# Two edits in a conformer decoder trunk on one core: an unused tile of 256 in place of 384 bytes, and a half layer norm's mean and root computed in PSUM by column

## The chip, the cores and the metric

The kernel runs on one core of one Trainium2 chip. Its time is the device time of that core in microseconds (us); the reported time is the median over several executions. Before the change it is 1984.59 us, the median of 3 (1982.06 to 1985.19). TensorE (PE in the profile) multiplies matrices out of SBUF into PSUM; VectorE (DVE), ScalarE (ACT) and GpSimd (POOL) work element by element; the queue of SyncE (SP) issues most of the DMAs. SBUF and PSUM both have 128 partitions; the addresses below are bytes within a partition.

## The reference

Two macaron layers over 512 tokens of 1024 channels, in fp32. Layer 0 mixes tokens with a convolution, layer 1 with stick-breaking attention; each layer has a half-step gated feed-forward block before and after its mixer.

```python
for layer in range(2):
    h = h + 0.5 * swiglu_ffn(rms_norm(h, ffn1_norm[layer]), ...)     # 1024 -> 2816 -> 1024
    u = rms_norm(h, mix_norm[layer])
    if layer == 0:                                                   # conformer_conv
        a, gate = split(u @ w_pw1 + b_pw1); c = a * sigmoid(gate)
        c = causal_depthwise_conv(c, w_dw, width=31) + b_dw
        c = silu(layer_norm(c, ln_g, ln_b))                          # mean and variance over channels
        h = h + c @ w_pw2 + b_pw2
    else:
        h = h + stick_breaking_attention(u @ wq, k, v) @ wo          # 16 heads of 64
    h = h + 0.5 * swiglu_ffn(rms_norm(h, ffn2_norm[layer]), ...)
    if layer == 0: k, v = split(rms_norm(h, kv_norm) @ w_kv)
return rms_norm(h, final_norm)
```

## The kernel before

The activations stand transposed: 8 chunks of 128 channels, each a tile of 128 partitions by 512 tokens. Each fp32 operand of a matmul is split into a high and a low part (`split`: ACT casts to the high part, DVE subtracts it for the low part), and a product takes three matmuls (`mm3`, L325 to L327): weight high by x high, weight high by x low, weight low by x high. The weight is the stationary operand (128x128, loaded by PEld), the activation the moving one (128x512).

There are four feed-forward blocks (`ffn`, called here blocks 0 to 3). Each runs in thirds of 8, 8 and 6 hidden chunks f. For each f two products, gate and up, go into PSUM tiles `pg` (8 input chunks by 3 matmuls each); DVE and ACT make the hidden tile from them and split it into `hhi` and `hlo`. After a third, each of the 8 output chunks d takes a product `pd` over the third's hidden tiles. The moving operand of `pg` is `xhi`/`xlo` of a `Norm`, that of `pd` is `hhi`/`hlo`. Weights come in units of 128x1024 (`unit`, `fetch`) through three buffers each of `raw`, `whi` and `wlo`.

Where tiles lie: pools are laid out one after the other, `const`, `wp` (weights), `xp` (the `xhi`/`xlo` of blocks 0, 2 and 3), `tp`, then the pools of each stage. `lean(tp, LEAN_TP)` reserves a tile in `tp` that nothing writes or reads; `LEAN_DG` does so in a later pool. What lies behind it in `tp`, and each later pool, starts higher by its size. In the built program the tiles of interest start, modulo 512 bytes:

| tiles | before | after |
|---|---|---|
| `whi`, `wlo`; `xhi`, `xlo` of blocks 0, 2, 3 and of the mixers (up to byte 105536) | 64 | 64 |
| `xhi`, `xlo` of block 1 (pool `x2`); `hhi`, `hlo`, `tg`, `tu` (all blocks); `kvh`, `kvl`, `oh`, `ol` (attention) (from byte 107968 on) | 192 | 64 |
| `qs`, `ks`, `sh`, `sl`, `wh`, `wl`, `vs` (attention); `sq` and diagonals (`dg`) in `tp` | 448 | 320 |
| `gl`, `glh`, `gll` (convolution, four buffers each) | 0, 128, 256, 384 | 64, 192, 320, 448 |

The convolution stage is not left to the scheduler but written as steps for a planner (`Plan`): each step has an engine, an estimated duration, its buffers and a rank, and `issue` orders the steps by a list schedule over these estimates. First come the projections `pa` with the gate (`gl`); then, for each channel chunk, 31 taps shared between PE (diagonal matrices `d` into PSUM tiles `pc`), ACT and POOL (`pr`, `ws`) and DVE (L690, adding onto `pc`). The last three chunks are done in two halves of 256 tokens, so that the layer norm of the first half, `layer_norm(0, ..)`, can begin while the taps of the second half still run.

`layer_norm(h, ..)` sums over channels with matmuls: `ms` holds the mean of 2 x 128 tokens in 2 columns of a PSUM tile, `mq` the mean square. DVE copies the mean to the SBUF tile `sm` (L713). `row` then brings two columns onto all partitions: split them (L719, L720), scale an identity by each part on ACT (`dg_lm`, `dg_lr`, L726) and multiply by ones on PE (`pb_lm`, `pb_lr`, L728). `variance` (L736 to L740) squares the mean, subtracts, clamps, and takes the inverse root with `inv_root` (L360 to L370: two integer instructions, then three rounds of three). With both rows there, DVE and POOL subtract the mean (L746, L748), DVE multiplies by the root (L756), ACT applies Silu (L757) and casts (L759), and `second` multiplies by the weights of the second projection (`pp`).

Attention is left to the scheduler, which orders it by its own model of time: projections (`pk`, `pq`, `pv`), 16 heads (`z`, `av`), and the output projection (`po`).

Of the kernel before, what the change touches and what calls it, by code (L numbers as in the profile page):

```python
# [30 lines left out]
LEAN_TP, LEAN_DG = 384, 64  # L31
# [151 lines left out]
def decoder_kernel(ctx, tc, xin, gu, dna, dnb, pw1, pw2, kq, wv, wo, out):  # L183
# [343 lines left out]
    with ExitStack() as c:  # L527
# [125 lines left out]
        def depthwise(ch, sl, rank):  # L653
# [18 lines left out]
            for t in range(n_pe, n_pe + n_pool):  # L672
                q = ch * KW + t
                x, g = lambda t=t: gl()[:, t + h : t + sl.stop], col("w_dw", q)
                if t > n_pe:
                    pr = held("pr", f"pr{q}_{h}", [P, T], F32)
                    add("A", 0.6 * f + 0.08 * half, lambda pr=pr, x=x, g=g: A.activation(pr()[:, at0], x(), AF.Copy, scale=g),  # L677
# [3 lines left out]
                else:  # L681
                    add("A", 0.6 * f + 0.08 * half, lambda x=x, g=g: A.activation(
# [21 lines left out]
        def layer_norm(h, rank):  # L704

            sl, n = TOKENS[h], T // 2
            sm = cv.tile([P, 8], F32, name=f"sm{h}")
            mean, var, root = sm[:, 0:2], sm[:, 2:4], sm[:, 4:6]
            y7, sq = ("y", NC - 1, sl.start), ends[h]
            ms, mq = bank(f"ms{h}", 2), bank(f"mq{h}", 2)  # L710
            add("PE", 1.0, lambda: token_sums(ms(), dsum[:, sl], y[NC - 1]()[:, sl]), r=[f"dsum{h}", y7], w=[ms], rank=rank)
            add("PE", 1.0, lambda: token_sums(mq(), dsq[:, sl], sq()[:, sl]), r=[f"dsq{h}", sq], w=[mq], rank=rank)
            add("V", 0.2, lambda: V.tensor_copy(mean, ms()), r=[ms], w=[("mean", h)], rank=rank)  # L713

            def row(name, small, key):
# [403 lines left out]
```

## Time and profile before

| | |
|---|---|
| time, median of 3 | 1984.59 us |
| the profiled execution: its own time | 1984.59 us |
| its span in the profile | 1982.8 us |
| PE busy | 1938.9 us, 98% |
| DVE busy | 1089.9 us, 55% |
| ACT busy | 787.8 us, 40% |
| POOL busy | 278.4 us, 14% |

Busy shares are means over stages with different limits. A matmul's record lasts longer than the distance to the next matmul's start, since they are pipelined, so a sum of records says little and starts say more. The stages, in us from the span's start: block 0 to 372, convolution to 583, block 1 to 953, block 2 to 1316, attention to 1625, block 3 to the end.

### The profile page before, as it was taken

To read this page: it belongs to the slowest core of one execution; us is meant where nothing else is said; L and a number is where in the kernel's file an instruction comes from. 1 tells how busy PE (TensorE), PEld (TensorE's weight loads), DVE (VectorE), ACT (ScalarE), POOL (GpSimd) and SP (SyncE) were. 2 spreads that over 40 slices of the span, in tenths; PEclk is the share of its full clock that TensorE was granted. 3 is DMA by queue.
4 is the path that set the end of the run, shared out by engine and by line. 5 is a ranking of instruction groups with operands and counts; after the bars stand their busy time and mean duration, and the time that the engine had idled before them with its cause. 6 is when DMAs were issued, how large, how long until landed. Compare 5 with 4: busy or idle time off the path is not lost.

```text
span 1982.8 us, 23270 instructions
## 1 busy us (share of the span) xinstructions
PE 1938.9 (98%) x8991; PEld 1594.9 (80%) x8993; DVE 1089.9 (55%) x1646; ACT 787.8 (40%) x1222; POOL 278.4 (14%) x261
## 2 busy tenths in 40 slices
PE   8999999999799999999999999999999999999997
PEld 6888888888788888888888888888888688888885
DVE  6444534599754434345743443467989754344344
ACT  5424323667543222223422322346777633222222
POOL 0212202099500000000000000003453100000000
PEclk9999999999899999999999999999999999999998
DMA  5757746443243232322333333242323132332321
GB/s 195 242 172 241 270 144 230 166 159 128 107 160 96 94 91 92 96 93 89 105 97 94 97 97 95 76 157 77 86 76 93 57 96 96 96 96 87 105 83 66
DMA packets 69630, 237.62 MB, mean 120 GB/s; under 512 B 7952, under 2 KB 8080, under 8 KB 69520
## 3 DMA queue, kind: packets, MB, share of 16 engines
q1 hardware_dynamic: 62032, 209.93, 33.1%
q10 hardware_dynamic: 7488, 26.22, 3.6%
q8 instruction: 70, 1.15, 0.2%
q14 instruction: 40, 0.33, 0.1%
HBM read 202.56 MB, written 29.36 MB: 117 GB/s over the span
## 4 chain that ended last, share of the span: by engine, by line
PE 88%; DVE 5%; ACT 3%; issue 1%; POOL 1%; DMA 1%; SPq 0%; DVEq 0%; POOLq 0%; ACTq 0%
PE pg L327 16%; PE pg L325 16%; PE pg L326 16%; PE pd L327 8%; PE pd L326 8%; PE pd L325 8%; PE z L946 1%; DVE pc L690 1%; PE pa L326 1%; PE pa L327 1%; PE pa L325 1%; PE po L325 1%; PE po L326 1%; PE po L327 1%; POOL ws L679 1%
## 5 line engine op out<-in xcount | busy, mean ns | idle before, releaser
L234 ACT CAST whi<-raw 128x1024 fp32r<-128x1024 f32 (+2 forms) x305 | 313.0, 1028 | 940.8 <-PE pg L326 376.9
L325 PE MATMUL pg<-xhi_f,whi 128*128 128x512 f32 x1408 | 550.3, 391 | 4.2 <-ACT xhi_f L390 1.7
L326 PE MATMUL pg<-xlo_f,whi 128*128 128x512 f32 x1408 | 550.1, 391 | 1.6 <-DVE xlo_f L391 1.6
L327 PE MATMUL pg<-xhi_f,wlo 128*128 128x512 f32 x1408 | 550.0, 391 | 0.1
L235 DVE TENSOR_TENSOR wlo<-raw,whi 128x1024 fp32r<-128x1024 f32 (+2 forms) x305 | 368.6, 1210 | 63.9 <-ACT whi L234 63.6
L325 PEld LDWEIGHTS pg<-xhi_f,whi 128*128 128x128 f32 x1408 | 264.3, 188 | 64.0 <-ACT whi L234 3.9
L326 PEld LDWEIGHTS pg<-xlo_f,whi 128*128 128x128 f32 x1408 | 264.3, 188 | 60.1 <-DVE xlo_f L391 3.0
L327 PEld LDWEIGHTS pg<-xhi_f,wlo 128*128 128x128 f32 x1408 | 264.3, 188 | 57.6 <-DVE wlo L235 0.8
L326 PE MATMUL pd<-hlo,whi 128*128 128x512 f32 x704 | 277.4, 395 | 0.0
L327 PE MATMUL pd<-hhi,wlo 128*128 128x512 f32 x704 | 276.8, 395 | 0.0
L325 PE MATMUL pd<-hhi,whi 128*128 128x512 f32 x704 | 276.7, 395 | 0.0
L464 DVE SCALAR_TENSOR_TENSOR xpar<-pd,xpar 128x512 f32<-128x512 f32 x96 | 66.0, 691 | 256.9 <-PE pd L327 256.9
L448 DVE TENSOR_TENSOR tu<-pg,r_f 128x512 f32<-128x512 f32 x88 | 60.8, 691 | 265.8 <-PE pg L327 265.6
L446 DVE TENSOR_TENSOR tg<-pg,r_f 128x512 f32<-128x512 f32 x88 | 60.8, 691 | 179.9 <-PE pg L327 179.9
L326 PEld LDWEIGHTS pd<-hlo,whi 128*128 128x128 f32 x704 | 132.1, 188 | 32.2
L327 PEld LDWEIGHTS pd<-hhi,wlo 128*128 128x128 f32 x704 | 132.1, 188 | 32.0
L325 PEld LDWEIGHTS pd<-hhi,whi 128*128 128x128 f32 x704 | 132.2, 188 | 32.0
L845 POOL TENSOR_SCALAR_AFFINE_SELECT tri<-ones 128x128 f32<-128x128 f32 x1 | 0.3, 294 | 725.3 <-DVE tu L449 725.3
L235 POOL TENSOR_TENSOR plo<-praw,phi 128x1024 fp32r<-128x1024 f32 x24 | 57.5, 2400 | 283.4 <-ACT phi L234 281.8
L679 POOL TENSOR_TENSOR ws<-ws,pr 128x256 f32<-128x256 f32 (+1 forms) x90 | 90.8, 1019 | 28.3 <-ACT pr L677 24.6
L690 DVE SCALAR_TENSOR_TENSOR pc<-gl,xpar,pc 128x512 f32<-128x512 f32 (+1 forms) x154 | 91.9, 639 | 2.8 <-PE pc L669 1.1
L234 ACT CAST hhi<-tu 128x512 fp32r<-128x512 f32 x88 | 54.9, 624 | 67.1 <-DVE tu L449 67.1
(262 smaller groups left out, 2489.6 us busy)
## 6 DMA issues: line engine op xcount, KB each, us to landing
raw<-in_gu_dram SPq DMA_DIRECT2D x175, 512.0 KB, 3.5
raw<-in_dna_dram SPq DMA_DIRECT2D x64, 512.0 KB, 3.5
whi<-aparth SPq DMA_DIRECT2D x29, 512.0 KB, 3.5
wlo<-apartl SPq DMA_DIRECT2D x29, 512.0 KB, 4.4
praw<-in_pw_dram SPq DMA_DIRECT2D x24, 512.0 KB, 4.0
aparth<-phi ACTq DMA_DIRECT2D x24, 512.0 KB, 2.7
apartl<-plo ACTq DMA_DIRECT2D x24, 512.0 KB, 3.8
raw<-in_dnb_dram SPq DMA_DIRECT2D x32, 384.0 KB, 3.1
```

The lines of the kernel that those rows point to most:

```text
L234: ins = A.copy(dst_hi, src)
L235: (G if on_pool else V).tensor_sub(dst_lo, src, dst_hi.bitcast(F32))
L325: PE.matmul(ps, w[0], x[0], start=first, stop=False)
L326: PE.matmul(ps, w[0], x[1], start=False, stop=False)
L327: PE.matmul(ps, w[1], x[0], start=False, stop=last)
L446: V.tensor_mul(tg, pt[0], rb)
L448: V.tensor_mul(tu, pt[1], rb)
L464: V.scalar_tensor_tensor(res[d], pd, 0.5, res[d], op0=ALU.mult, op1=ALU.add)
L679: add("G", 1.28 * f + 0.1 * half, lambda pr=pr: G.tensor_add(accp, accp, pr()[:, at0]), r=[pr], w=[at_], rank=rank)
L690: add("V", 0.66 * f + 0.06 * half, lambda x=x, q=q: V.scalar_tensor_tensor(pc(), x(), q, pc(), op0=ALU.mult, op1=ALU.add), r=[gl], w=[pc], ...
L845: G.affine_select(out=tri, in_=ones, compare_op=ALU.is_ge, fill=0.0, base=0, pattern=[[-1, P]], channel_multiplier=1,)
L946: PE.matmul(dst, st, m[:, a:b], start=False, stop=True, skip_group_check=True)
```

## The change

`LEAN_TP` goes from 384 to 256. `layer_norm` loses the SBUF tile `sm` and its copy: `mq` becomes a PSUM tile of 8 columns, of which 0 and 1 take the mean square, 2 and 3 the variance, 4 and 5 the root, 6 and 7 a scratch value. `row` takes its two columns from PSUM (`ms`, and columns 4 and 5 of `mq`). The products of two columns become two instructions on one column each, with the other factor as a scalar by partition, also in PSUM. `inv_root`, still used by the RMS norms, has its first two instructions in a function of their own. Five estimates of the planner change (one is shown).

```diff
-LEAN_TP, LEAN_DG = 384, 64
+LEAN_TP, LEAN_DG = 256, 64
...
+    def first_root(y, v):
+
+        V.tensor_scalar(y.bitcast(I32), v.bitcast(I32), 1, None, op0=ALU.logical_shift_right)
+        V.tensor_scalar(
+            y.bitcast(I32), y.bitcast(I32), -1, 0x5F3759DF, op0=ALU.mult, op1=ALU.add
+        )
...
-                add("A", 0.54, do, w=[d], rank=rank)
+                add("A", 0.6, do, w=[d], rank=rank)
...
-            sm = cv.tile([P, 8], F32, name=f"sm{h}")
-            mean, var, root = sm[:, 0:2], sm[:, 2:4], sm[:, 4:6]
...
-            ms, mq = bank(f"ms{h}", 2), bank(f"mq{h}", 2)
+            ms, mq = bank(f"ms{h}", 2), bank(f"mq{h}", 8)
...
-            add("V", 0.2, lambda: V.tensor_copy(mean, ms()), r=[ms], w=[("mean", h)], rank=rank)
...
-                    V.tensor_copy(parts[:, :2], small)
-                    V.tensor_sub(parts[:, 2:], small, parts[:, :2].bitcast(F32))
+                    V.tensor_copy(parts[:, :2], small())
+                    V.tensor_sub(parts[:, 2:], small(), parts[:, :2].bitcast(F32))
...
-            lm = row("lm", mean, ("mean", h))
+            lm = row("lm", ms, [ms])
...
             def variance():
-                V.tensor_mul(root, mean, mean)
-                V.tensor_sub(var, mq(), root)
+                var, root, t = (mq()[:, a : a + 2] for a in (2, 4, 6))
+                one = [slice(j, j + 1) for j in range(2)]
+                for j in one:
+                    V.tensor_scalar_mul(root[:, j], ms()[:, j], ms()[:, j])
+                for j in one:
+                    V.tensor_scalar(var[:, j], root[:, j], -1.0, mq()[:, j], op0=ALU.mult, op1=ALU.add)
                 V.tensor_scalar(var, var, 0.0, LN_EPS, op0=ALU.max, op1=ALU.add)
-                inv_root(root, var, f"ln{h}")
-            add("V", 2.9, variance, r=[mq, ("mean", h)], w=[("root", h)], rank=rank)
-            lr = row("lr", root, ("root", h))
+                first_root(root, var)
+                for _ in range(3):
+                    for j in one:
+                        V.tensor_scalar_mul(t[:, j], root[:, j], root[:, j])
+                    for j in one:
+                        V.tensor_scalar(t[:, j], t[:, j], var[:, j], -0.5, op0=ALU.mult, op1=ALU.mult)
+                    for j in one:
+                        V.tensor_scalar(root[:, j], t[:, j], 1.5, root[:, j], op0=ALU.add, op1=ALU.mult)
+            add("V", 3.4, variance, r=[ms], w=[mq], rank=rank)
+            lr = row("lr", Buf("-", lambda: mq()[:, 4:6]), [mq])
```

On DVE, the first layer norm from the mean's arrival to the first round of the root, before (`sm` is the SBUF tile, a tap of the second half's convolution reads `gl` into `pc_256`):

```order
L713 COPY sm_2889<-ms_4309 128x2 [waits PE_49]
L690 SCALAR_TENSOR_TENSOR pc_256_4166<-gl_3758,xpar,pc_256_4166 128x256 [waits DVE_49]
L719 CAST dp_lm_2890<-sm_2889 128x2 [waits DVE_49]
L720 TENSOR_TENSOR dp_lm_2890<-sm_2889,dp_lm_2890 128x2 [waits DVE_49]
L690 SCALAR_TENSOR_TENSOR pc_256_4166<-gl_3758,xpar,pc_256_4166 128x256
L737 TENSOR_TENSOR sm_2889<-sm_2889 128x2
L738 TENSOR_TENSOR sm_2889<-mq_4322,sm_2889 128x2 [waits DVE_49,PE_49]
L739 TENSOR_SCALAR sm_2889<-sm_2889 128x2 [waits DVE_49]
L363 TENSOR_SCALAR sm_2889<-sm_2889 128x2 [waits DVE_49]
L364 TENSOR_SCALAR sm_2889<-sm_2889 128x2 [waits DVE_49]
L368 TENSOR_TENSOR rt_ln_4347<-sm_2889 128x2 [waits DVE_49]
L369 SCALAR_TENSOR_TENSOR rt_ln_4347<-sm_2889,rt_ln_4347 128x2 [waits DVE_49]
```

and the same place now:

```order
L722 CAST dp_lm_2889<-ms_4315 128x2 [waits PE_49]
L723 TENSOR_TENSOR dp_lm_2889<-ms_4315,dp_lm_2889 128x2 [waits DVE_49]
L694 SCALAR_TENSOR_TENSOR pc_256_4159<-gl_3759,xpar,pc_256_4159 128x256
L743 TENSOR_SCALAR mq_4328<-ms_4315 128x1 [waits PE_49]
L743 TENSOR_SCALAR mq_4328<-ms_4315 128x1 [waits DVE_49]
L745 TENSOR_SCALAR mq_4328<-mq_4328 128x1 [waits DVE_49] x2
L746 TENSOR_SCALAR mq_4328<-mq_4328 128x2 [waits DVE_49]
L362 TENSOR_SCALAR mq_4328<-mq_4328 128x2 [waits DVE_49]
L363 TENSOR_SCALAR mq_4328<-mq_4328 128x2 [waits DVE_49]
L750 TENSOR_SCALAR mq_4328<-mq_4328 128x1 [waits DVE_49] x2
L752 TENSOR_SCALAR mq_4328<-mq_4328 128x1 [waits DVE_49] x2
L754 TENSOR_SCALAR mq_4328<-mq_4328 128x1 [waits DVE_49] x2
```

The copy is gone, one tap moved ahead of the mean's split, and the products by columns stand in pairs. On PE, the end of the first layer norm's place in the queue, before (`pc_256` are the last diagonal taps of the second half):

```order
L728 MATMUL pb_lm_4372<-dg_lm_0_4339,onesr 128x256
L325 MATMUL pc_256_4257<-glh_4024,d_4239 128x256
L326 MATMUL pc_256_4257<-gll_4039,d_4239 128x256
L327 MATMUL pc_256_4257<-glh_4024,d_4239 128x256
L728 MATMUL pb_lm_4372<-dg_lm_1_4359,onesr 128x256
L669 MATMUL pc_256_4257<-y0h,mshift 128x256
L728 MATMUL pb_lr_4406<-dg_lr_0_4396,onesr 128x256
L728 MATMUL pb_lr_4406<-dg_lr_1_4399,onesr 128x256
L325 MATMUL pp_0_4436<-shi_4419,whi_3767 128x256
```

and now:

```order
L325 MATMUL pc_256_4249<-glh_4022,d_4267 128x256
L326 MATMUL pc_256_4249<-gll_4040,d_4267 128x256
L327 MATMUL pc_256_4249<-glh_4022,d_4267 128x256
L731 MATMUL pb_lm_4383<-dg_lm_0_4339,onesr 128x256
L673 MATMUL pc_256_4249<-y0h,mshift 128x256
L731 MATMUL pb_lm_4383<-dg_lm_1_4379,onesr 128x256
L731 MATMUL pb_lr_4416<-dg_lr_0_4406,onesr 128x256
L731 MATMUL pb_lr_4416<-dg_lr_1_4409,onesr 128x256
L325 MATMUL pp_0_4446<-shi_4430,whi_3765 128x256
```

The last three diagonal taps moved ahead of the mean's row; in both orders no tap is left between the rows of mean and root but the closing one with `mshift`. In attention, PE's queue in the first heads, before (`pq` a projection, `z` the scores of a head):

```order
L327 MATMUL pq_10586<-xhi_mix_4_9878,wlo_10457 128x512
L325 MATMUL pq_10586<-xhi_mix_5_9911,whi_10456 128x512
L326 MATMUL pq_10586<-xlo_mix_5_9912,whi_10456 128x512
L327 MATMUL pq_10586<-xhi_mix_5_9911,wlo_10457 128x512
L946 MATMUL z_0_10275<-sh_0_10295,ntri 128x512
L325 MATMUL pq_10586<-xhi_mix_6_9944,whi_10456 128x512
L326 MATMUL pq_10586<-xlo_mix_6_9945,whi_10456 128x512
L327 MATMUL pq_10586<-xhi_mix_6_9944,wlo_10457 128x512
L946 MATMUL z_1_10281<-sh_1_10321,ntri 128x384
```

and now:

```order
L960 MATMUL z_0_10291<-sh_0_10311,ntri 128x512
L327 MATMUL pq_10602<-xhi_mix_4_9894,wlo_10473 128x512
L325 MATMUL pq_10602<-xhi_mix_5_9927,whi_10472 128x512
L326 MATMUL pq_10602<-xlo_mix_5_9928,whi_10472 128x512
L327 MATMUL pq_10602<-xhi_mix_5_9927,wlo_10473 128x512
L960 MATMUL z_0_10291<-sl_0_10312,ntri 128x512
L960 MATMUL z_0_10291<-sh_0_10311,none 128x256
L960 MATMUL z_0_10291<-sl_0_10312,none 128x256
L325 MATMUL pq_10602<-xhi_mix_6_9960,whi_10472 128x512
```

The head's matmuls stand four places earlier among those of the projection; such shifts run through the whole of attention.

## Rows read from the trace of the kernel before

**Rows 1.** The page's chain of work that ended last, by engine.

```profile
PE 88%; DVE 5%; ACT 3%; issue 1%; POOL 1%; DMA 1%; SPq 0%; DVEq 0%; POOLq 0%; ACTq 0%
```

**Rows 2.** Stretches: length, busy us (instructions) by engine, clock, DMA share, GB/s.

```profile
28.00:372.00 344.00, 344.00 (x1504) 281.99 (x1503) 160.53 (x199) 123.31 (x144) 57.55 (x24) 1.00 0.61 205
372.00:583.00 211.00, 195.42 (x1134) 173.11 (x1132) 167.32 (x333) 139.98 (x306) 121.37 (x129) 0.96 0.40 148
583.00:953.00 370.00, 370.00 (x1591) 298.03 (x1592) 167.51 (x217) 105.14 (x129) 0.00 (x0) 1.00 0.30 94
...
1316.00:1625.00 309.00, 299.32 (x1569) 247.34 (x1571) 242.48 (x419) 193.38 (x352) 93.41 (x92) 0.98 0.28 81
```

**Rows 3.** PE groups by line, block 1: count, busy us, mean ns, idle.

```profile
L325 PE MATMUL pg<-xhi_f,whi 128*128 128x512 f32 x352 | 138.9, 395 | 0.0
...
L326 PE MATMUL pd<-hlo,whi 128*128 128x512 f32 x176 | 69.4, 395 | 0.0
```

**Rows 4.** PE groups by line, block 2.

```profile
L325 PE MATMUL pg<-xhi_f,whi 128*128 128x512 f32 x342 | 133.2, 389 | 0.0
...
L325 PE MATMUL pd<-hhi,whi 128*128 128x512 f32 x176 | 69.2, 395 | 0.0
```

**Rows 5.** PE timeline, first matmuls of thirds in blocks 1 and 2: start, duration.

```profile
711.55 0.40 PE L325 MATMUL pg<-xhi_f,whi 128*128 128x512 f32 x1
...
801.15 0.40 PE L325 MATMUL pd<-hhi,whi 128*128 128x512 f32 x1
...
845.95 0.40 PE L325 MATMUL pg<-xhi_f,whi 128*128 128x512 f32 x1
...
1080.06 0.39 PE L325 MATMUL pg<-xhi_f,whi 128*128 128x512 f32 x1
...
1167.12 0.40 PE L325 MATMUL pd<-hhi,whi 128*128 128x512 f32 x1
```

**Rows 6.** PE's waits in the convolution stage: us in total, times, longest.

```profile
PE pb_lr L728 <- ACT dg_lr L726: 7.6, 1, 7.6
```

**Rows 7.** DVE timeline around the first layer norm: start, us, instructions.

```profile
492.56 8.45 DVE L690 SCALAR_TENSOR_TENSOR pc<-gl,xpar,pc 128x256 f32<-128x256 f32 x21
...
502.69 0.15 DVE L713 COPY sm<-ms 128x2 f32<-128x2 f32 x1
...
504.97 0.37 DVE L737 TENSOR_TENSOR sm<-sm 128x2 f32<-128x2 f32 x1
...
511.96 0.65 DVE L370 SCALAR_TENSOR_TENSOR sm<-rt_ln,sm 128x2 f32<-128x2 f32 x1
...
512.86 0.16 DVE L719 CAST dp_lr<-sm 128x2 fp32r<-128x2 f32 x1
```

**Rows 8.** ACT and POOL timelines in the same stretch.

```profile
507.85 0.51 ACT L677 ACTIVATE pr<-gl,xpar 128x256 f32<-128x256 f32 x1 [0.25 <-POOL ws L679]
513.05 1.28 ACT L726 ACTIVATE dg_lr<-ident,dp_lr 128x128 fp32r<-128x128 f32 x4 [4.69 <-DVE dp_lr L719]
...
510.52 2.07 POOL L679 TENSOR_TENSOR ws<-ws,pr 128x256 f32<-128x256 f32 x3
```

**Rows 9.** DVE timeline around the second layer norm.

```profile
536.75 0.16 DVE L720 TENSOR_TENSOR dp_lm<-sm,dp_lm 128x2 fp32r<-128x2 f32 x1
536.83 0.15 DVE L737 TENSOR_TENSOR sm<-sm 128x2 f32<-128x2 f32 x1
...
539.62 0.16 DVE L370 SCALAR_TENSOR_TENSOR sm<-rt_ln,sm 128x2 f32<-128x2 f32 x1
```

**Rows 10.** Stretches behind the first layer norm's wait, columns as in rows 2.

```profile
514.00:523.50 9.50, 7.47 (x31) 6.89 (x32) 9.37 (x25) 8.35 (x22) 1.60 (x2) 0.50 0.01 2
523.50:527.00 3.50, 3.50 (x31) 3.50 (x31) 1.86 (x6) 1.04 (x3) 2.90 (x5) 1.00 0.00 0
```

**Rows 11.** PE's waits in attention, the longest.

```profile
PE pq L325 <- DVE qt L908: 3.1, 1, 3.1
```

**Rows 12.** The stretch around that wait, columns as in rows 2.

```profile
1340.00:1350.00 10.00, 6.87 (x19) 5.08 (x18) 4.91 (x7) 3.93 (x6) 0.00 (x0) 0.66 0.39 106
```

More of the change, by code (lines that the diff above doesn't have):

```diff
@@ L358, in token_sums @@
                           start=i + b == 0, stop=i == len(src) - 1, skip_group_check=True)
-    def inv_root(y, v, name):
-        t = tp.tile([P, v.shape[-1]], F32, name=f"rt_{name}", tag="rt", bufs=1)
+    def first_root(y, v):
         V.tensor_scalar(y.bitcast(I32), v.bitcast(I32), 1, None, op0=ALU.logical_shift_right)
@@ L366, in inv_root @@
         )
+    def inv_root(y, v, name):
+        t = tp.tile([P, v.shape[-1]], F32, name=f"rt_{name}", tag="rt", bufs=1)
+        first_root(y, v)
         for _ in range(3):
@@ L676, in depthwise @@
                     pr = held("pr", f"pr{q}_{h}", [P, T], F32)
-                    add("A", 0.6 * f + 0.08 * half, lambda pr=pr, x=x, g=g: A.activation(pr()[:, at0], x(), AF.Copy, scale=g),
+                    add("A", 0.6 * f + 0.1 * half, lambda pr=pr, x=x, g=g: A.activation(pr()[:, at0], x(), AF.Copy, scale=g),
                         r=[gl], w=[pr], rank=rank)
@@ L681, in depthwise @@
                 else:
-                    add("A", 0.6 * f + 0.08 * half, lambda x=x, g=g: A.activation(
+                    add("A", 0.6 * f + 0.1 * half, lambda x=x, g=g: A.activation(
                         accp, x(), AF.Identity, scale=g, bias=col("b_dw", ch)), r=[gl], w=[at_], rank=rank)
@@ L706, in layer_norm, with row @@
             sl, n = TOKENS[h], T // 2
-            sm = cv.tile([P, 8], F32, name=f"sm{h}")
-            mean, var, root = sm[:, 0:2], sm[:, 2:4], sm[:, 4:6]
             y7, sq = ("y", NC - 1, sl.start), ends[h]
-            ms, mq = bank(f"ms{h}", 2), bank(f"mq{h}", 2)
+            ms, mq = bank(f"ms{h}", 2), bank(f"mq{h}", 8)
             add("PE", 1.0, lambda: token_sums(ms(), dsum[:, sl], y[NC - 1]()[:, sl]), r=[f"dsum{h}", y7], w=[ms], rank=rank)
-            add("PE", 1.0, lambda: token_sums(mq(), dsq[:, sl], sq()[:, sl]), r=[f"dsq{h}", sq], w=[mq], rank=rank)
-            add("V", 0.2, lambda: V.tensor_copy(mean, ms()), r=[ms], w=[("mean", h)], rank=rank)
-            def row(name, small, key):
+            add("PE", 1.0, lambda: token_sums(mq()[:, 0:2], dsq[:, sl], sq()[:, sl]), r=[f"dsq{h}", sq], w=[mq], rank=rank)
+            def row(name, small, r):
                 parts = tp.tile([P, 4], F32R, name=f"dp_{name}{h}", tag=f"dp{name}{h}", bufs=1)
@@ L718, in part @@
                 def part():
-                    V.tensor_copy(parts[:, :2], small)
-                    V.tensor_sub(parts[:, 2:], small, parts[:, :2].bitcast(F32))
-                add("V", 0.4, part, r=[key], w=[("parts", name, h)], rank=rank)
+                    V.tensor_copy(parts[:, :2], small())
+                    V.tensor_sub(parts[:, 2:], small(), parts[:, :2].bitcast(F32))
+                add("V", 0.5, part, r=r, w=[("parts", name, h)], rank=rank)
                 for i in range(2):
@@ L756, in layer_norm @@
                 add("V", 0.36, lambda yc=yc: V.tensor_mul(yc(), yc(), lr()), r=[lr], w=[yt], rank=rank)
-                add("A", 0.4, lambda yc=yc, ch=ch: A.activation(
+                add("A", 0.5, lambda yc=yc, ch=ch: A.activation(
                     yc(), yc(), AF.Silu, scale=col("ln_g", ch), bias=col("ln_b", ch)), w=[yt], r=["silu"], rank=rank)
-                add("A", 0.4, lambda yc=yc, hi=hi: A.copy(hi()[:, sl], yc()), r=[yt], w=[("shi", ch, h)] + [hi] * (h == 0), rank=rank)
+                add("A", 0.32, lambda yc=yc, hi=hi: A.copy(hi()[:, sl], yc()), r=[yt], w=[("shi", ch, h)] + [hi] * (h == 0), rank=rank)
                 add("V", 0.36, lambda yc=yc, hi=hi, lo=lo: V.tensor_sub(lo()[:, sl], yc(), hi()[:, sl].bitcast(F32)),
```

## The prediction

> **What bounds the kernel now.** I read the chain of work that ended last, then the busy time by stage, then TensorE's starts in each feed-forward block, then the one long wait.
>
> The chain is 88% TensorE [rows 1]. By stage [rows 2], TensorE is busy without a gap in the feed-forward blocks (344.00 of 344.00 us in the first, 370.00 of 370.00 in the second), while the convolution stage leaves 211.00 − 195.42 = 15.6 us idle and attention 309.00 − 299.32 = 9.7. So in four fifths of the span the time is the number of matmuls times the distance between their starts, and only something that changes that distance counts. In the convolution and attention stages DVE is loaded too (167 of 211 us, 242 of 309).
>
> The distance is not the same everywhere. In block 1 a 128x512 matmul lasts 395 ns in both pg and pd [rows 3]; in block 2 pg lasts 389 and pd 395 [rows 4]. Records overlap, so I take the distance from starts. Eight units f make 8 x 2 x 8 x 3 = 384 pg matmuls, eight units d make 8 x 8 x 3 = 192 pd matmuls. In block 1, pg from 711.55 to 801.15 is 89.60 us, 233.3 ns each; the pd behind it, to 845.95, is 44.80 us, again 233.3. In block 2, pg from 1080.06 to 1167.12 is 87.06 us, 226.7 ns [rows 5]. Same engine, shape, clock (1.00 in both), same weights' place; block 1's xhi and xlo begin at 192 modulo 512, block 2's at 64, and hhi and hlo (pd's moving operand) at 192 in every block. So a moving operand at 192 costs 6.6 ns a matmul against one at 64, or something that goes with it does.
>
> **The change part by part.**
>
> *The unused tile.* It puts hhi, hlo, and block 1's xhi and xlo at 64. pd: 4 blocks x 22 x 8 x 3 = 2112 matmuls; pg of block 1: 44 x 8 x 3 = 1056. Together 3168 x 6.6 ns = 20.9 us, all on the path since TensorE has no gap there. What could be late next: DVE has 167.51 busy of 370 us and the DMA engines a share of 0.61 at most in these stages [rows 2], so neither takes over for 2%. Bounds: 0 (the distance goes with another property than the start) to 20.9.
>
> In attention pk and po (192 matmuls each) go from 192 to 64 too: at 6.6 ns the 384 are worth 2.5 us. po has little beside it, pk is mixed with the heads. The tiles of the heads go from 448 to 320, for which no row has a price. I take 1.5 us, between 0 and 2.5. gl, read by DVE and ScalarE, moves through the same four remainders in another order; I take nothing.
>
> *The layer norm's statistics.* For the first half of the tokens TensorE waits once, 7.6 us, for the diagonals of the root (pb_lr) [rows 6]. What it waits for is a string of DVE instructions on two columns [rows 7]: the copy of the means at 502.69, the squaring at 504.97, and the split of the root at 512.86. From 504.97 to 512.61 stand 14 tiny instructions, most at 0.65 to 0.68 us. In the second half the same 14 take 536.83 to 539.78, 0.20 each [rows 9]. The difference is POOL: it adds 256 columns at 0.69 us each until 512.6 in the first half [rows 8] and nothing in the second; DVE's instruction with SBUF on both sides goes through once per POOL instruction. Those with an operand in PSUM do not wait: the copy from ms at 502.69 took 0.15 beside a busy POOL [rows 7].
>
> After the change all of it stands in PSUM. The copy goes; the two instructions of the mean's split read PSUM, 0.2 each; one tap of 8.45 / 21 = 0.40 follows [rows 7]; the string then begins at 502.69 + 0.4 + 0.4 = 503.5, 1.5 earlier. It has 11 pairs of columns and 3 of both, 25 in place of 14. No row shows a PSUM-to-PSUM instruction of one column with a scalar by column. From below: an independent one follows its forerunner after 0.08 (536.75 to 536.83) [rows 9], 25 x 0.08 = 2.0 us. From above: a tap, which reads and writes PSUM, takes a scalar by column and waits for its forerunner, but over 256 columns, 0.40 [rows 7]: 10.0 us. I take 0.20 + 0.08 + 0.07 for a pair and 0.2 for a single, 11 x 0.35 + 0.6 = 4.45 us, nearest to the second half's row. The string ends at 507.95, and with one subtraction of 0.33 before it the root's split starts at 508.3, 4.6 earlier than 512.86.
>
> What is late next is ScalarE. In the new order two products pr stand ahead of the root's diagonals, and pr waits for POOL (507.85, idle 0.25 before it) [rows 8]: 507.85 + 0.51 + 0.69 = 509.05 in place of 513.05. So the gain is 4.0 us, from −1.0 (string of 10.0: 503.5 + 10.0 + 0.33 = 513.8 against 512.86) to 4.3, ScalarE's floor with a shorter wait for POOL. Behind the wait TensorE ran at a granted clock of 0.50, that is at 1.2 GHz: 31 matmuls in 7.47 busy us where the next 31 took 3.50 [rows 10]. It had stood idle before that; with about half the idle I count 1.0 of these 4.0 us back (0 to 4).
>
> By the Trainium skill, SBUF — State Buffer, section "Who interferes with whom", DVE instructions with two SBUF inputs, and those in a two-port mode, wait for the whole of a GpSimd instruction that reads SBUF, and PSUM operands are outside that. By that rule none of the 25 waits, and the trace agrees so far (0.15 us for the copy from PSUM, 0.65 for SBUF to SBUF); were the rule narrower than that, rival 2 is what follows.
>
> In the second half pb_lr has no wait (the one wait of 7.6 is the first half's) [rows 6]: TensorE has pp matmuls beside it, and a string 1.5 us longer than 2.95 hides there; without cover it would cost 1.5.
>
> *The planner's numbers.* They move instructions by a few places from the convolution's start. Until the first layer norm TensorE or DVE is full either way, and each executes the same instructions less the copy; I take nothing, ±1.
>
> *Attention's order.* The scheduler emits its matmuls in another order, though the code there is untouched; SP's queue holds the same DMAs, some of the qs and ks copies one weight load later or earlier. Nothing says which order is better; 0, and ±6 for the bounds, about what the one long pause there costs now (5.7 us, worked out under rival 3).
>
> The sum: 20.9 + 1.5 + 4.0 + 1.0 = 27.4 us. The profiled execution had a span of 1982.8 us and took 1984.59, the median of the runs shown. 1984.6 − 27.4 = **1957.2**. Its own range: with everything at its good end 20.9 + 2.5 + 4.3 + 4 + 1 + 6 = 38.7, 1946; with the string at its bad end and attention 6 us worse, 20.9 − 1.0 − 1 − 6 = 12.9, 1972. As these don't fall together I take 1948 to 1971.
>
> **Rivals.**
>
> 1. *The distance does not come from the start modulo 512.* All tiles that are read at 226.7 ns lie below byte 105536 of the partition, all at 233.3 above 107968, so the trace alone does not part the start from the region. Against it: the two blocks differ by 6.6 ns and agree with each other to 0.1 within each place, and of a cost that grows with the address pd shows nothing, with 395 ns for hhi and for the higher hlo [rows 3, 4]. Then only the layer norm counts: 1984.6 − 5.0 = 1979.6. The Trainium skill speaks for this rival: TensorE: Matmul & The Clock Gate, section "Wait — 56ns, not 53.3ns?", gives a warm distance that hangs on the column count alone, 215.7 ns for 512, and knows no address. The trace does not agree: its two distances, 226.7 and 233.3, differ at one clock and one column count.
>
> 2. *The tiny instructions wait for POOL in PSUM too.* One per POOL instruction, 0.69 each, from 503.5 until POOL runs dry at 512.6: 13 go by then, the other 12 at 0.2 end at 515.0, 2.4 later than now. 1984.6 − 20.9 − 1.5 + 2.4 = 1964.6. Against it: the 0.15 us of the copy from ms.
>
> 3. *Attention's new order opens pauses.* One is there now: TensorE waits 3.1 us for qt, and from 1340 to 1350 the granted clock averages 0.66 and 19 matmuls pass where 10 us hold 44 [rows 11, 12]; 25 x 0.227 = 5.7 us lost. The sixteen heads could each have one. It decides from five new pauses on (28 us, all of the gain); six make 1957.2 + 34 = 1991, slower. For it: DVE stands at 242 of 309 us and the projections that fill the heads' waits have moved [rows 2]. Against: TensorE idles 9.7 us in the whole stage now, and its longest wait is that one [rows 2, 11].
>
> **How the numbers follow.** Forecast 0.83 (1957), rival 1 0.09 (1980), rival 2 0.04 (1965), rival 3 0.04 (1991). About 0.2%, 4 us, is what a measurement of this kernel can tell from no change. The forecast and rival 2 are faster; rival 1 lies on that bound, so I split it: faster 0.91, same 0.05, slower 0.04. The range 1948 to 1971 leaves out rivals 1 and 3 and some of the forecast's own ends, under 0.2.
>
> **What would show it.** pd and block 1's pg at 389 ns, and their 192 and 384 matmuls in 43.5 and 87.1 us; the wait at pb_lr near 3.6 us in place of 7.6, its string in PSUM at 0.15 to 0.2 an instruction while POOL adds; half clock behind it for less than before; attention's stage within 6 us of 309. pd left at 395 ns would make the prediction wrong by 20; a string at 0.65 an instruction, or a wait above 3 us in attention that was not there, by less.

## The result, and the profile after

The changed kernel takes 1960.95 us (median of 4, 1960.59 to 1961.26) against 1984.89 (1982.06 to 1985.38) for the kernel before: a ratio of 0.9882, 95% interval 0.9865 to 0.9899. The forecast was 1957.2, so the time came out faster by 23.9 us where 27.4 was forecast. The profiled execution has a span of 1958.9 us, 23.9 less than before.

To see where they come from I cut both spans at the same matmuls. In the PE timeline after the change (start, duration) the convolution stage begins with the first `pa`, attention with the first `pv`, block 3 with its first `pg`:

```profile
372.20 0.39 PE L325 MATMUL pa<-xhi_mix,whi 128*128 128x512 f32 x1
...
1291.68 0.28 PE L325 MATMUL pv<-whi,kvh 128*128 128x256 f32 x1
...
1581.05 0.47 PE L325 MATMUL pg<-xhi_f,whi 128*128 128x512 f32 x1 [0.88 <-ACT whi L234]
```

The same matmuls of before stood at 375.96, 1310.80 and 1601.54, and the first `pg` of block 1 at 575.77, now at 570.70. The lengths between them, in us (the stages named ahead were cut more roughly: attention's 1316 to 1625 in [rows 2] holds 23 us of block 3, the convolution's 372 to 583 holds 7 us of block 1):

| stage | before | after | difference | forecast |
|---|---|---|---|---|
| block 0, to the first `pa` | 375.96 | 372.20 | −3.8 | |
| convolution, to block 1's first `pg` | 199.81 | 198.50 | −1.3 | −5.0 |
| blocks 1 and 2, to the first `pv` | 735.03 | 720.98 | −14.1 | |
| attention, to block 3's first `pg` | 290.74 | 289.37 | −1.4 | −1.5 |
| block 3 to the end of the span | 381.26 | 377.85 | −3.4 | |

The four feed-forward blocks gave 3.8 + 14.1 + 3.4 = 21.2 us, forecast 20.9. Attention gave what was forecast, though not for the reason given, as the runs below show. The convolution stage gave 1.3 of 5.0, and that is nearly all of the difference between forecast and time.

The feed-forward blocks first. PE's groups in block 1 after the change (count, busy us, mean ns, idle) answer to [rows 3]:

```profile
L325 PE MATMUL pg<-xhi_f,whi 128*128 128x512 f32 x352 | 136.9, 389 | 0.0
L326 PE MATMUL pd<-hlo,whi 128*128 128x512 f32 x176 | 68.3, 389 | 0.0
```

The PE timeline of a third there (the first `pg`, the first `pd`, the next third's first `pg`) answers to [rows 5]:

```profile
702.72 0.39 PE L325 MATMUL pg<-xhi_f,whi 128*128 128x512 f32 x1
...
789.76 0.39 PE L325 MATMUL pd<-hhi,whi 128*128 128x512 f32 x1
...
833.28 0.39 PE L325 MATMUL pg<-xhi_f,whi 128*128 128x512 f32 x1
```

Records of 395 ns became 389, the 384 matmuls `pg` take 87.04 us and the 192 `pd` 43.52, both 226.7 ns each. By stage (length, then busy us and instructions of PE, PEld, DVE, ACT, POOL, then clock, DMA share, GB/s; compare [rows 2]) TensorE still has no gap there:

```profile
372.00:577.50 205.50, 192.13 (x1115) 170.23 (x1114) 164.43 (x350) 136.36 (x299) 120.91 (x125) 0.96 0.41 146
577.50:938.00 360.50, 360.50 (x1595) 298.57 (x1594) 167.50 (x217) 105.30 (x130) 0.00 (x0) 1.00 0.31 97
...
1291.70:1581.00 289.30, 278.46 (x1507) 232.56 (x1505) 234.40 (x400) 187.34 (x347) 94.01 (x92) 0.99 0.28 83
```

Then the layer norm. TensorE's wait for the root's row, one of 7.6 us before [rows 6], is now two, 5.0 us in the first half and 2.2 in the second (us in total, times, longest):

```profile
PE pb_lr L731 <- ACT dg_lr L729: 7.2, 2, 5.0
```

DVE's timeline shows why the first is no shorter (compare [rows 7]):

```profile
499.01 0.15 DVE L722 CAST dp_lm<-ms 128x2 fp32r<-128x2 f32 x1
...
499.87 0.50 DVE L743 TENSOR_SCALAR mq<-ms 128x1 f32<-128x1 f32 x2
500.41 0.50 DVE L745 TENSOR_SCALAR mq<-mq 128x1 f32<-128x1 f32 x2
500.94 0.17 DVE L746 TENSOR_SCALAR mq<-mq 128x2 f32<-128x2 f32 x1
501.14 0.17 DVE L362 TENSOR_SCALAR mq<-mq 128x2 int32<-128x2 int32 x1
...
505.82 0.50 DVE L754 TENSOR_SCALAR mq<-mq 128x1 f32<-128x1 f32 x2
...
506.55 0.15 DVE L722 CAST dp_lr<-mq 128x2 fp32r<-128x2 f32 x1
```

while POOL adds throughout:

```profile
496.78 7.65 POOL L683 TENSOR_TENSOR ws<-ws,pr 128x256 f32<-128x256 f32 x10
504.38 2.76 POOL L762 TENSOR_TENSOR y<-y,lms 128x256 f32<-128x256 f32 x4
```

Nothing in the string waits for POOL: an instruction on two columns follows the last after 0.20 us (500.94, 501.14). But a pair of single columns takes 0.53 (499.87 to 500.41), 11 pairs 5.9, and the whole string 499.87 to 506.32 = 6.45 us. In the changed kernel's program each of the string's instructions behind the first waits for the one right before it, so the second of a pair waits for the first, although they work on different columns; a pair is two steps of 0.27 us, one after the other. In the second half, where POOL never stood in the way, the string takes the same 6.45 in place of the 2.95 that followed from [rows 9]:

```profile
529.74 0.50 DVE L743 TENSOR_SCALAR mq<-ms 128x1 f32<-128x1 f32 x2 [0.54 <-PE mq L357]
...
535.69 0.50 DVE L754 TENSOR_SCALAR mq<-mq 128x1 f32<-128x1 f32 x2
...
536.42 0.15 DVE L722 CAST dp_lr<-mq 128x2 fp32r<-128x2 f32 x1
```

ScalarE, meanwhile, had done its products at 504.97 and stood idle for DVE's split:

```profile
504.46 0.51 ACT L681 ACTIVATE pr<-gl,xpar 128x256 f32<-128x256 f32 x1 [0.29 <-POOL ws L683]
506.74 1.28 ACT L729 ACTIVATE dg_lr<-ident,dp_lr 128x128 fp32r<-128x128 f32 x4 [1.77 <-DVE dp_lr L722]
```

And TensorE's granted clock fell to 0.50 again, 1.2 GHz: behind the first wait for some 10 us, for 3.4 us at 524.2, and then, where `pp` is dense, for 3.4 us at 537.9, right behind the second wait. There 17 matmuls pass in 3.4 us where the next 3.4 hold 31 (columns as above):

```profile
503.50:513.75 10.25, 4.04 (x15) 3.45 (x16) 9.85 (x34) 7.02 (x19) 5.67 (x9) 0.51 0.00 0
...
537.90:541.30 3.40, 3.40 (x17) 3.40 (x17) 2.87 (x9) 1.81 (x6) 0.00 (x0) 0.50 0.00 0
541.30:544.70 3.40, 3.40 (x31) 3.40 (x31) 2.89 (x9) 3.40 (x9) 0.00 (x0) 1.00 0.00 0
```

One wait is gone that no term of the forecast had. Before, TensorE stood 1.2 us ahead of block 1's first `pg`:

```profile
PE pg L325 <- DVE xpar L806: 1.2, 1, 1.2
```

In the changed kernel that `pg` follows the last `pp` after 0.12 us.

In attention the longest wait stands where it stood [rows 11], and no pause like it was added (the next is 1.4 us):

```profile
PE pq L325 <- DVE qt L922: 3.1, 1, 3.1
PE z L960 <- POOL sl L998: 1.4, 1, 1.4
```

### The profile page after: what moved, and what is told of

Read it like the earlier page. It is cut to its first block, busy times and chain, and to the rows that moved or that the text cites. A ratio compares the mean times of both kernels' runs of the same rounds, so it can differ in the third digit from the quotient of the medians.

```text
span 1958.9 us, 23277 instructions
## 1 busy us (share of the span) xinstructions
PE 1916.1 (98%) x8993; PEld 1594.7 (81%) x8993; DVE 1089.1 (56%) x1666; ACT 786.5 (40%) x1222; POOL 278.7 (14%) x261
## 4 chain that ended last, share of the span: by engine, by line
PE 92%; DVE 4%; ACT 2%; DMA 1%; issue 1%; POOL 0%; SPq 0%; DVEq 0%; ACTq 0%
PE pg L325 16%; PE pg L327 16%; PE pg L326 16%; PE pd L325 8%; PE pd L326 8%; PE pd L327 8%; PE z L960 1%; PE pa L325 1%; PE pa L327 1%; PE pa L326 1%; PE po L325 1%; DMA wlo<-apartl 1%; PE po L326 1%; PE po L327 1%; PE pv L325 1%
## 5 line engine op out<-in xcount | busy, mean ns | idle before, releaser
L326 PE MATMUL pd<-hlo,whi 128*128 128x512 f32 x704 | 273.2, 389 | 0.0
L327 PE MATMUL pd<-hhi,wlo 128*128 128x512 f32 x704 | 272.6, 389 | 0.0
L325 PE MATMUL pd<-hhi,whi 128*128 128x512 f32 x704 | 272.6, 389 | 0.0
L325 PEld LDWEIGHTS pd<-hhi,whi 128*128 128x128 f32 x704 | 132.1, 188 | 27.4
```

The lines of the kernel that those rows point to most:

```text
L325: PE.matmul(ps, w[0], x[0], start=first, stop=False)
L326: PE.matmul(ps, w[0], x[1], start=False, stop=False)
L327: PE.matmul(ps, w[1], x[0], start=False, stop=last)
```

## The experiments

The theory after this reading: the shift is worth all of the gain; the layer norm's edit wins 2.6 us at the first wait and loses it again at the second, by half clock and in attention. The table gathers stage lengths of the profiles that bear on it, cut as above, with the waits at `pb_lr` and, for both stages, the total time at half clock; the runs follow in order.

| kernel | waits at `pb_lr` | half clock in the convolution | convolution | half clock in attention | attention |
|---|---|---|---|---|---|
| before | 7.6 | 17.1 | 199.8 | 10.2 | 290.7 |
| changed kernel | 5.0, 2.2 | 17.1 | 198.5 | 6.8 | 289.4 |
| the same, again | 4.9, 0 | 20.5 | 198.4 | 10.2 | 291.4 |
| the same without the unused tile | 5.0, 0.8 | 13.7 | 197.4 | 6.8 | 289.6 |
| shift alone | 7.6, 0 | 13.7 | 198.0 | 6.8 | 287.8 |
| layer norm alone | 4.8, 0.8 | 17.1 | 196.8 | 10.2 | 292.7 |
| old planner numbers | 3.6, 2.2 | 17.1 | 198.5 | 6.8 | 290.2 |
| second half in SBUF | 4.8, 0 | 17.1 | 195.5 | 6.8 | 284.9 |
| two wide in PSUM | 2.9, 0 | 17.1 | 195.3 | 6.8 | 287.7 |
| two wide, then SBUF | 2.9, 0 | 17.1 | 194.9 | 6.8 | 287.9 |

Three more kernels further down (the weights moved, starts 0 and 128) have the changed kernel's order of matmuls in the convolution stage and took 196.6, 198.7 and 198.4 us there. With the table's rows of that order (the changed kernel twice, without the unused tile, layer norm alone) the stage of one order ranges from 196.6 to 198.7, one profile each and at different starts.

### The shift alone

```diff
 (kernel before)
-LEAN_TP, LEAN_DG = 384, 64
+LEAN_TP, LEAN_DG = 256, 64
```

> The kernel before with the unused tile of 256 bytes and nothing else; every engine executes the same instructions in the same order as before. Theory (the moving operand's start sets the distance): pd in all blocks and block 1's pg go from 233.3 to 226.7 ns, 3168 x 6.6 = 20.9 us, and attention's pk and po give 0 to 2.5: 1961.5 to 1964, and the convolution stage stays within 1 us of before. Rival 1 (the distance goes by the order of the program or by something else that the layer norm's edit brought): pd stays at 395 ns, 1984.9 within 4.

1959.23 us (1957.88 to 1962.73) against 1981.96, ratio 0.9887 (0.9873 to 0.9900): as much as the whole change. The difference, 22.7 us, is inside the 20.9 to 23.4 expected; before ran 3 us quicker beside it than in the runs of the result, and ratios, not times, are compared from here on. Every matmul of the blocks is at 389 ns. The hidden tiles moved by 128 bytes and stayed in their region, so the forecast's rival 1 (the region, not the start) has fallen. Attention gave 3.0 us at an unchanged order, but not all of it comes from the starts. Between the same two matmuls of a projection `pq`, whose operands' starts did not move, 1.2 us are won where the kernel before is at half clock and this one no longer is; before first, then the shift alone (columns as in the windows above):

```profile
1346.91:1349.74 2.83, 2.83 (x9) 2.20 (x8) 0.00 (x0) 0.00 (x0) 0.00 (x0) 0.54 0.35 88
```

```profile
1327.06:1328.66 1.60, 1.60 (x8) 1.32 (x7) 0.00 (x0) 0.00 (x0) 0.00 (x0) 1.00 0.61 158
```

The other 1.7 come mostly where `pk` and `po` stand, 1.1 of them in the closing `po`. The heads show no share of their own: `sh` and `ntri`, `qs` and `ks`, `wl` and `vs` moved together, and behind a 128x512 matmul of `sh` and `ntri` the next one starts after 234 ns (the median) in both kernels. The convolution stage gave 1.8, outside the 1 us expected, with 3.4 us less at half clock, which at half speed is worth 1.7: no more than that can be said of it.

### The layer norm alone

```diff
 (changed kernel)
-LEAN_TP, LEAN_DG = 256, 64
+LEAN_TP, LEAN_DG = 384, 64
```

> The changed kernel with the unused tile back at 384 bytes: layer norm in PSUM and the planner's numbers alone. Theory (the layer norm was mis-sized: pairs of columns at 0.53 us, both strings 6.4 us): two waits at pb_lr of about 5.0 and 2.2 us, the convolution stage 1 to 1.5 us shorter than before, attention within 1: 1983 to 1984. Rival (the layer norm is worth the forecast 5.0 us, and the tiles of the convolution, moved in their remainders by the shift, took 3.7 of it back): the convolution stage 5 us shorter, 1980.

1983.91 us against 1981.96, ratio 1.0005 (0.9995 to 1.0015): nothing. The convolution stage is 3.0 us shorter, between the two expectations, and attention 1.9 longer. Of the 3.0, 2.8 is the first wait (7.6 to 4.8); the second came out at 0.8 where 2.2 was expected, and the 1.2 us ahead of block 1 are gone as in the changed kernel.

### The second half in SBUF, and two wide in PSUM

The first takes `variance` in the second half back to two columns in SBUF; the second keeps PSUM, but puts one operand of each instruction into SBUF, so that it works on two columns at once:

```diff
 (second half in SBUF)
+                if h:
+                    V.tensor_copy(mean, ms())
+                    V.tensor_mul(root, mean, mean)
+                    V.tensor_sub(var, mq()[:, 0:2], root)
...
+                    inv_root(root, var, "ln1")
 (two wide in PSUM: rs, vs in SBUF; root, t in PSUM)
+                for i in range(3):
+                    V.tensor_mul(t, rs, root)
+                    V.scalar_tensor_tensor(t, t, -0.5, vs, op0=ALU.mult, op1=ALU.mult)
+                    if i < 2:
+                        V.scalar_tensor_tensor(root, t, 1.5, rs, op0=ALU.add, op1=ALU.mult)
+                    V.scalar_tensor_tensor(rs, t, 1.5, rs, op0=ALU.add, op1=ALU.mult)
```

> The changed kernel, but the second half's mean square and root in SBUF on two columns as before (14 instructions and the copy of the mean at 0.2 us, about 3.0 in place of 6.4); the first half stays in PSUM by column. Theory (the second string lost its cover): no wait of 2.2 us at the second pb_lr, no half clock behind it, the convolution stage 2.2 to 4 us shorter than in the changed kernel, 1957 to 1959. Rival (what comes behind that wait, the copies of wlo and the casts to shi, is late anyway): the waits of pp grow by what pb_lr's loses, and the stage keeps its length within 0.7 us, 1961.

> The changed kernel, but in both halves mean square and root on two columns at once, each instruction with one operand in PSUM and the other in SBUF (the root kept in both): 19 instructions in place of 25. Theory (an instruction with a scalar by column in PSUM costs 0.27, one on two columns 0.2, and an operand in PSUM is enough to pass POOL): string 3.8 to 4.0 us in both halves, first wait at pb_lr 2.5 to 3.5 in place of 5.0, second 0 to 0.5 in place of 2.2, the stage 3 to 6 us shorter than in the changed kernel, 1955 to 1958. Rival a (with one operand in SBUF the instruction still waits for POOL): the first half's string at 0.65 each, 12 us, and the time 6 us above the changed kernel's, 1967. Rival b (ScalarE, or what comes behind, is late next): strings short, but the stage within 1 us of the changed kernel's.

With SBUF in the second half: 1952.78 us, ratio 0.9853 (0.9840 to 0.9866). DVE's second string, from the copy at 529.11 to 532.36, takes 3.25 us:

```profile
529.11 0.15 DVE L744 COPY sm<-ms 128x2 f32<-128x2 f32 x1
...
532.20 0.16 DVE L374 SCALAR_TENSOR_TENSOR sm<-rt_ln,sm 128x2 f32<-128x2 f32 x1
```

Of TensorE's waits at `pb_lr` one is left:

```profile
PE pb_lr L731 <- ACT dg_lr L729: 4.8, 1, 4.8
```

The second wait is gone and the stage 3.0 us shorter than in the changed kernel, so its rival (what comes behind is late anyway) has fallen. Only 1.3 of the 3.0 are the string's for certain: in the second half the way from the first matmul of `ms` to that of `pb_lr` went from 9.84 to 8.56 us. The other 1.8 lie behind it, where the changed kernel was at half clock in dense `pp` and this one was not; against the shortest stage of the changed kernel's order, 196.6, the gain is 1.1. The rest of its gain, 4.5 us, was not expected: attention is shorter, and TensorE's matmuls there stand in an order that neither kernel had.

Two wide: 1955.75 us, ratio 0.9864 (0.9851 to 0.9878). The first string, 499.59 to 503.27, takes 3.7 us in place of 6.45, at 0.20 an instruction beside POOL, so rival a has fallen too:

```profile
499.59 0.15 DVE L746 COPY sm<-ms 128x2 f32<-128x2 f32 x1
...
501.31 0.17 DVE L755 SCALAR_TENSOR_TENSOR mq<-mq,sm 128x2 f32<-128x2 f32 x1
501.51 0.17 DVE L757 SCALAR_TENSOR_TENSOR mq<-mq,sm 128x2 f32<-128x2 f32 x1
...
503.11 0.16 DVE L758 SCALAR_TENSOR_TENSOR sm<-mq,sm 128x2 f32<-128x2 f32 x1
...
503.90 0.47 DVE L722 CAST dp_lr<-sm 128x2 fp32r<-128x2 f32 x1
504.40 0.64 DVE L723 TENSOR_TENSOR dp_lr<-sm,dp_lr 128x2 fp32r<-128x2 f32 x1
```

The last two rows are the counter-sample: the split of the root reads SBUF here, and beside POOL takes 0.47 and 0.64 where the changed kernel's, out of PSUM, takes 0.15 and 0.16; with POOL idle, the first of them out of SBUF took 0.16 as well [rows 7]. The first wait falls to 2.9 us, the second to none, the stage to 195.3. But a wait of 2.9 brings the same length at half clock as one of 7.6. The stretch behind it in this kernel (columns as in the windows above):

```profile
501.40:515.10 13.70, 8.09 (x32) 6.91 (x33) 13.07 (x41) 12.03 (x32) 8.79 (x13) 0.50 0.00 1
```

and in the one with the shift alone, whose wait is 7.6 us:

```profile
504.40:518.00 13.60, 5.74 (x23) 5.16 (x24) 13.24 (x34) 7.79 (x21) 4.56 (x8) 0.50 0.01 1
```

### The changed kernel again, and three other starts

> The changed kernel once more, beside its own runs of the kernel before, to see how far the convolution stage and the places at half clock vary from one execution to the next. Theory (where the half clock falls varies, and with it 1 to 2 us of the stage): the stage again 198.5 us within 2, attention 289.4 within 1 and 1.6 longer than with the shift alone, as the order of its instructions is the same; time 1959 to 1961.5, not below the shift alone. Rival (the layer norm's edit is worth 3 us of its own and the first profile fell in a bad place): the stage at 196 and the time 1957 or below.

1961.18 us (1960.45 to 1962.48), ratio 0.9890 (0.9873 to 0.9906): the theory's range. The convolution stage is within 0.1 us of the first profile, though in this execution the second wait is gone and 3.4 us more at half clock have taken its place. Attention came out at 291.4, outside the 289.4 within 1 that was expected; it holds 3.4 us more at half clock, so this term varies by some 2 us between executions.

Then the disputed start itself. One kernel moves the weights, too:

```diff
 (changed kernel)
+    lean(const, 128)
...
-LEAN_TP, LEAN_DG = 256, 64
+LEAN_TP, LEAN_DG = 128, 64
```

> The changed kernel with 128 unused bytes ahead of the weights and the unused tile at 128: whi, wlo and the xhi, xlo of blocks 0, 2, 3 now begin at 192 modulo 512, hhi, hlo and block 1's xhi, xlo at 64 as in the changed kernel. Theory (the moving operand's own start sets the distance): pg at 233.3 ns in blocks 0, 2 and 3 and 226.7 in block 1, pd at 226.7 everywhere; 3168 matmuls slower, 21 us, and about as much as 3 us in attention, 1980 to 1985. Rival 1 (what counts is that moving and stationary operand begin alike): pg of blocks 0, 2, 3 at 226.7, all pd at 233.3, and block 1's pg too. Rival 2 (the stationary operand's start counts): all at 233.3, 42 us longer, 2003.

Its one time is 1981.12. PE's groups in block 0, where `pg` reads `xhi` at 192 against weights at 192, and `pd` reads `hhi` at 64 against weights at 192 (its lines are one later):

```profile
L326 PE MATMUL pg<-xhi_f,whi 128*128 128x512 f32 x330 | 128.4, 389 | 0.0
...
L326 PE MATMUL pd<-hhi,whi 128*128 128x512 f32 x171 | 67.2, 395 | 0.0
```

That is the first rival, not the theory: a moving operand at 192 is quick, one at 64 is slow, and what decides is whether it begins like the weights. In block 1, where `xhi` begins at 64 against 192, `pg` too has 394 to 395, 232.4 ns from start to start. The time would not have told: 3168 slow matmuls by the theory, 3168 other ones by the rival.

The starts 0 and 128, with the weights at 64 again, by the unused tile at 192 and 320:

> The changed kernel with the unused tile at 192: hhi, hlo and block 1's xhi, xlo begin at 0 modulo 512, the rest as in the changed kernel. Theory (a start of 64 is quick and others are slow): 233.3 ns, 1982. Rival (192 is the bad place, or the second quarter of 256 is good and 0 as good or better): 226.7 ns or less, 1961 or less.

> The changed kernel with the unused tile at 320: hhi, hlo and block 1's xhi, xlo begin at 128 modulo 512. Theory (64 alone is quick): 233.3 ns, 1982. Rival a (a start in the lower half of each 256 is quick, 128 and 192 slow): 233.3 too, where start 0 is at 226.7. Rival b (192 is the bad place): 226.7, 1961.

One time each: 1982.18 and 1970.06. Start 0 has 394 ns throughout. Start 128 lies between, which none of the expectations had, and its groups in block 1 differ among themselves:

```profile
L327 PE MATMUL pg<-xhi_f,wlo 128*128 128x512 f32 x353 | 138.9, 394 | 0.0
L326 PE MATMUL pg<-xlo_f,whi 128*128 128x512 f32 x353 | 138.2, 392 | 0.0
L325 PE MATMUL pg<-xhi_f,whi 128*128 128x512 f32 x352 | 136.6, 389 | 0.0
```

From start to start that is 229.0 ns on the mean. Which of the three groups is slow is not fixed: in block 0 of the same kernel `pd` has 394 for `hhi` by `whi`, 388 for `hlo` by `whi` and 392 for `hhi` by `wlo`. The last start has the unused tile left out:

> The changed kernel without the unused tile: hhi, hlo and block 1's xhi, xlo begin at 320 modulo 512, that is 256 from the weights' 64. Theory a (what counts is the difference from the weights' start modulo 256): 226.7 ns and 1961. Theory b (the difference modulo 512): another distance, 229 to 233.3 ns, 1969 to 1982.

1959.59, with 226.7 ns everywhere:

```profile
L326 PE MATMUL pg<-xlo_f,whi 128*128 128x512 f32 x352 | 136.9, 389 | 0.0
```

So 256 bytes from the weights' start is as good as none. Of the differences moving minus weights, modulo 256: 0 gives 226.7 ns, 64 gives 229.0, 128 and 192 give 232.4 to 233.3. That is read off `pg` and `pd`, at these four differences; why it is so, no run shows.

### The old numbers, and both string repairs together

```diff
 (changed kernel; one of five estimates)
-                add("A", 0.6, do, w=[d], rank=rank)
+                add("A", 0.54, do, w=[d], rank=rank)
```

> The changed kernel with the five estimates of the planner as they were; its attention has the changed kernel's order. Theory (they only move instructions by a few places): the convolution stage 198.4 us within 1, the two waits at pb_lr 5.0 and 2.2 within 0.5, attention 289 to 291.5. Rival (the estimates, not the strings, took the gain of the first half back): the stage at 196 or below, or the second wait gone.

One time of 1961.22, the stage 198.5, attention 290.2. The waits are 3.6 and 2.2: the first missed the expectation by 1.4 us, yet the stage is the same to 0.1. The wait ahead of block 1 is back, with 1.1 us, so the five numbers move waits about, but in sum they took nothing back.

The last kernel has two wide in PSUM for the first half and SBUF for the second.

> The changed kernel, the first half's root two wide with one operand in PSUM (19 instructions), the second half's in SBUF as before (15). Its attention has the order of the kernel before, matmul for matmul. Theory (the stage is set by the two waits at pb_lr, attention by its order): first wait 2.9 us, none in the second half, the convolution stage 194 to 196 us, attention 287.7 within 0.5, so 1953 to 1956: 5 to 8 below the changed kernel, and not below the kernel with SBUF in the second half alone, whose attention took 284.9. Rival (half clock behind the first wait, 13.65 us in every run but two, sets the stage, not the waits): the stage as long as in the kernel with SBUF in the second half, 195.5, although the first wait is 1.9 shorter.

1954.75 us (1953.70 to 1956.03), ratio 0.9866 (0.9850 to 0.9883). Waits, attention and time came as the theory had them. The stage, 194.9, is 0.6 us shorter than with SBUF in the second half alone, while the first wait is 1.9 shorter. Followed from matmul to matmul, the other 1.3 go in pieces: 0.4 right behind, where `pp` now waits for DVE's `slo`, 0.3 at half clock, 0.2 around the second sums, 0.4 in the last microseconds of the stage. So the rival, half clock, explains a small part of it.

Attention's order can be read off these kernels. Both with two wide have TensorE's attention in the order of the kernel before, and take 287.7 and 287.9, like the shift alone at 287.8. The changed kernel's own order, with the same 6.8 us at half clock, took 289.4, 290.2 and (start 320) 289.6, a mean of 289.7; with 10.2 at half clock it took 291.4. The third order, of SBUF in the second half, took 284.9 with 6.8. Orders that nobody chose thus lie 5 us apart. Why one is better than another I have not tried to find out.

The quickest kernel is the one with SBUF in the second half, 1952.78. Its interval (0.9840 to 0.9866) lies below that of the shift alone (0.9873 to 0.9900) and touches the changed kernel's first one (0.9865 to 0.9899) at its end.

## Why the prediction was right, and where not

**The distance.** 20.9 us forecast, 21.2 measured, and the thirds in 87.04 and 43.52 us as written. The term held; its reason only in part. It named the operand's own start modulo 512 "or something that goes with it", and it is the latter, the difference from the weights' start: in all blocks of before the weights began at 64. The rule that was read off two blocks would have got the kernel with moved weights wrong, block by block. The Trainium skill (TensorE: Matmul & The Clock Gate, section "Wait — 56ns, not 53.3ns?") lets the distance hang on columns alone; at 512 columns and a granted clock of 1.00 these runs have 226.7, 229.0 and 233.3 ns.

**Attention.** 1.5 forecast for the starts, 0 for the order; 1.4 measured. The starts gave about 1.7 (shift alone), as forecast. But the order took 1.9 back (289.7 − 287.8 at like half clock), inside its ±6, and 3.4 us less at half clock, for which the sum had no term, gave 1.2 in the shift alone and stand in the changed kernel too. That the total fits is luck: two terms that were put at nothing largely cancelled.

**The layer norm** is the step that was mis-sized. "0.20 + 0.08 + 0.07 for a pair" was 0.53, the string 6.45 in place of 4.45, inside its bounds of 2.0 to 10.0, and the first wait fell by 2.6 us in place of 4.0. What failed is the 0.08: the second of a pair was counted as independent of the first, and in the kernel's queue it waits for it, as all the others of the string wait for the one before. With the wait, 0.20 and the 0.07 that was allowed for the scalar stand twice in a pair, near the 0.53 measured. That 0.07 fits both instructions; whether it is the scalar, its place in PSUM or the single column that costs it, no run parts. Two columns at once stayed at 0.20. ScalarE's floor, which the prediction called late next, was not reached; the products `pr` were done by 504.97, and ScalarE stood 1.77 us idle before the root's diagonals. Rival 2 had 0.04 and fell: nothing waited for POOL. The rule weighed there (the Trainium skill, SBUF — State Buffer, section "Who interferes with whom") agrees with these rows: 0.15 us for the split out of PSUM, 0.47 and 0.64 for the same out of SBUF.

**The second half.** "A string 1.5 us longer than 2.95 hides there": it came out 3.5 longer and did not hide. From the first matmul of `ms` to that of `pb_lr` the changed kernel takes 527.86 to 537.71, 9.85 us, in other executions of that second string 9.84 to 10.5, and with SBUF there 7.1 to 8.6. The price that the prediction set on lost cover, 1.5, is near what was lost, 9.84 − 8.55 = 1.3 with like half clock and 9.85 − 7.1 = 2.8 at most; it stood outside the sum.

**Half clock.** 1.0 us was counted back for a shorter wait; nothing came. The stretch behind the first wait kept 13.7 us in most profiles (10.2 in the others), with 7.6 us of wait and with 2.9. What varies is where the rest of it falls: in dense `pp` it cost 14 matmuls in 3.4 us (17 against 31), 14 x 3.4 / 31 = 1.5 us; where TensorE would wait next it can cost little (the changed kernel again: 3.4 us more of it, no second wait, the stage as long).

**The sum.** 21.2 for the blocks + 1.4 in attention + 1.3 in the convolution stage = 23.9. In that 1.3 stand the first wait (2.6), the wait ahead of block 1 (1.2), the second (−2.2), and half clock and the rest (−0.3). Rivals 1 and 3 fell: the shift did all of its work, and no new pause above 1.4 us opened in attention.

## What to carry to other kernels

Where TensorE has no gap, compare the distance of matmuls between places with the same shape before touching anything else; if it differs, look at where both operands begin, moving and stationary, not at one of them. A fix for the half of the work where an engine stands in the way is applied to that half alone: the other half had the cheaper form already. Before two instructions are counted as overlapping, look in the queue whether the second waits for the first. When a scheduler orders a later stage, check by the instruction order whether an edit has moved it, before its difference is put down to the edit; and compare stages at like half clock, or cut at the same matmuls to see where the difference arises.

## What the runs showed that was not expected

- The distance of 128x512 matmuls depends on moving start minus weights' start modulo 256: 226.7 ns at 0, 229.0 at 64, 232.4 to 233.3 at 128 and 192. At 64 the three groups of a product have records of 388 to 389, 392 and 394 ns, and which group has which differs between block 0 and block 1.
- An instruction on one column whose scalar is a column in PSUM takes 0.27 us, one on two columns 0.20, waiting for its forerunner in both cases.
- A DVE instruction with one operand in SBUF and one in PSUM passes a busy POOL at 0.20 us; the split with SBUF alone took 0.47 and 0.64 in the same stretch.
- The length at half clock behind TensorE's wait did not follow the wait: 13.7 us behind 7.6 and behind 2.9, 10.2 behind the changed kernel's 5.0.
